# A hybrid decoder layer: one batch of row gathers cut four shorter, a Gelu in two halves, and other places for gathers and matmul chunks

## The chip, the cores and the metric

The kernel runs on one core of a Trainium2 chip. The number compared is device time in microseconds (us), taken over whole executions. The kernel before was timed three times: 1535.12, 1538.91 and 1541.09 us, median 1538.91 us. One further execution was profiled, and all rows below come from it.

The core's engines each work through their own list of instructions in order and meet at semaphores. PE multiplies matrices, DVE does element-wise work and reductions, ACT evaluates functions such as Exp, Ln and Gelu and copies results out of PE's accumulators, POOL issues the indirect gathers, and SP issues most plain transfers.

## The reference

The input is 512 tokens of width 1024. A layer has two halves, each closed by a LayerNorm over `alpha * x + f(x)`.

- The mixing half projects x to queries, keys and values. Eight heads (group A) are softmax attention over dilated windows: Exp of scores, divided by its sum. Eight heads (group B) are stick-breaking attention: `exp(log_sigmoid(z) + later)`, where `later` sums `log_sigmoid(-z)` over the later keys. So B needs Exp and Ln.
- The channel half looks up single-neuron experts. For each token, 8 heads each pick 16 of 16384 experts (128 in all, with softmax gates). Then

```
h   = einsum('td,ted->te', xb, u)        # u = rows of expert_u, 128 per token
act = gate * gelu(h, approximate=False)
y   = einsum('te,ted->td', act, vv)      # vv = rows of expert_v, 128 per token
```

## The kernel before

The 512 tokens are four blocks of 128. The channel half is computed in two ways:

- Blocks 0 and 1 gather. POOL fetches, for selection j of a block, one row of 1024 floats per token (512 KB in all). DVE uses it once: for `peer_u` rows it forms the dot product with x (L739, the result goes to column j of a tile `hs` of 128 columns), for `peer_v` rows it adds `hs[:, j] * row` to an accumulator (L750). A block has 128 gathers of u, then Gelu of `hs` (L741), a product with the gates (L745), then 128 gathers of v. Two blocks make 512 gathers. The generator `gathers` issues each up to 8 ahead of its use, and `done` counts uses.
- Blocks 2 and 3 are dense. PE multiplies x with all experts, 128 chunks of 128 (`h_part`, L847: 8 matmuls a chunk, each of which the trace shows as 2 records), ACT takes Gelu (L839), DVE multiplies with gates that were scattered to a dense table, and PE multiplies with `peer_v` (L1104). Up to 30 chunks (LEAD) are done ahead of the last loop, by `run_ahead(n)`, n matmuls at a time.

The order in time is this. First come the input projection and block 0's attention and routing (choice of its experts). Then `early = gathers(PRE0)` is mixed with the rest of the projection and with the A heads of blocks 1 and 2. From there on the order is written out by hand (`tc.manual_schedule()`):

1. The head pipeline: A heads of block 3, B heads of blocks 1, 2 and 3. One A head is scores on PE (L315), mask and minimum on DVE (L318), Exp on ACT (L321), transposes on PE (L325), a copy on ACT (L328), the product with v on PE (L331). One B head is scores on PE (L339, L341), Abs, Exp and Ln on ACT (L345, L346, L347), a sum on DVE (L349), sums over keys on PE (L351, L353), Exp on ACT (L355), the product with v on PE (L359). Heads overlap. `take(n)` puts n gather uses between the steps. The output projection and LayerNorm of blocks 1 and 2 are spread between the heads of blocks 2 and 3 (L497 on PE, L457 on DVE, then L160 on DVE, Ln and Exp on ACT at L161 and L162, L164 on DVE).
2. The output projection of block 3, then queries and scores of blocks 1 to 3 with DVE's top-16 searches, `run_ahead(1)` per step.
3. `route_steps(2)`, the routing of block 2, on DVE in 23 pieces, with gather uses and `run_ahead(8)` between the pieces. Near its end ACT takes an Exp (L681). It closes with three transposes on PE (L709).
4. The one-hot loop of 64 steps: DVE makes one-hot tiles (L798, L804), ACT scales them by the gates (L813), PE multiplies them (L819), and ACT copies the result out (L825). Beside it go gather uses, routing of blocks 3 and 1, and `run_ahead(2)` per step (3 in every eighth).
5. Chunks that are left of the 30, each with three gather uses, then the last loop over 128 chunks, in which the gathers that are left are spread.

ACT's functions come from tables. L176 loads one at the start, named `natural_log_exp_and_others`. After that the build puts an ACT_TABLE_LOAD ahead of a function that the table loaded last lacks, and the program and the trace show it under that function's line: the kernel before has 14 of them, one at L176, the next at L741.

Of the kernel before, what the change touches and what calls it, by code (L numbers as in the profile page):

```python
# [15 lines left out]
AF = mybir.ActivationFunctionType  # L16
# [57 lines left out]
LEAD = 30  # L74
KT = 6
MIXB = (5, 4, 2)
PRE0 = 68
QGATH = 3
QH = 1
PRE1 = 7  # L80
# [13 lines left out]
def build(ctx, nc, tc, a):  # L94
# [323 lines left out]
    def until(main, side, ratio):  # L418
        n = 0
        for _ in main:  # L420
            n += 1
            while n >= ratio:
                n -= ratio
                next(side, None)
# [5 lines left out]
    def run(*steps):  # L430
        ratio = steps[-1] if isinstance(steps[-1], tuple) else (1,) * len(steps)
        for _ in mix(*steps[:len(ratio)], ratio):
            pass

    def mix(*steps):
        ratio = steps[-1]
        live = [(s_, r) for s_, r in zip(steps, ratio)]
        while live:
            for s_, r in list(live):
                for _ in range(r):  # L440
                    if next(s_, s_) is s_:
                        live.remove((s_, r))
                        break
                    yield

    def head(steps, n):
        for _ in range(n):
            if next(steps, steps) is steps:
                return
            yield  # L450
# [283 lines left out]
    def gather_use(n, u):  # L734
        tb, kind, j = n // (2 * P), n // P % 2, n % P
        gate_, hs = sets[tb]
        x = x2[:, tb]
        if kind == 0:
            nc.vector.scalar_tensor_tensor(u, u, 1.0, x, op0=OP.mult, op1=OP.mult, accum_out=hs[:, j:j + 1])  # L739
            if j == P - 1:  # L740
                nc.scalar.activation(hs, hs, AF.Gelu)  # L741
                nc.vector.tensor_scalar_mul(x, x, ALPHA)
            return
        if j == 0:
            nc.vector.tensor_mul(hs, hs, gate_)  # L745
        if j == 1:
            nc.vector.tensor_scalar_mul(yg[0], u, hs[:, j:j + 1])
        else:
            acc = (x, yg[0])[j % 2]
            nc.vector.scalar_tensor_tensor(acc, u, hs[:, j:j + 1], acc, op0=OP.mult, op1=OP.add)  # L750
        if kind and j == P - 1:
            nc.vector.tensor_add(x, x, yg[0])
# [4 lines left out]
    def gathers(n):  # L757
        nonlocal done, issued
        while done < n:
            ahead_ = GB1 + GB2 if g2 else GB1  # L760
            while issued < min(done + ahead_ - 1, limit):
                gus[issued] = gather(issued)
                issued += 1
            gather_use(done, gus.pop(done))
            done += 1
            yield
# [27 lines left out]
    def one_hot_b(s):  # L794
        if s < NS:
            tb, t = steps[s]
            hot1[s] = gb.tile([P, P, TG], BF16, name="o1b", bufs=GBUF)
            nc.vector.tensor_tensor(hot1[s], gate[tb][0][:, None, t:t + TG].to_broadcast([P, P, TG]), iob, op=OP.is_equal)  # L798
# [32 lines left out]
    def load_u(c):  # L831
        if c < P:
            us[c] = wst.tile([P, KD, P], F32, name="w", bufs=WBUF)
            nc.sync.dma_start(us[c], a["uT"][c])

    def gelu(c, ps):
        if c % 2 == 0:
            gls[c // 2] = up.tile([P, 2, ND], F32, name="gl", bufs=LEAD // 2 + 2)
        nc.scalar.activation(gls[c // 2][:, c % 2], ps[:, :ND], AF.Gelu)  # L839
# [3 lines left out]
    def h_part(c, k0, k1):  # L843
        if k0 == 0:
            hps[c] = ps_h.tile([P, 512], F32, name="h", bufs=2)
        for k in range(k0, k1):
            nc.tensor.matmul(hps[c][:, :ND], us[c][:, k], xf[:, k], start=k == 0, stop=k == KD - 1)  # L847
        if k1 == KD:
            del us[c]
# [8 lines left out]
    def run_ahead(n):  # L858
        out = None
        for _ in range(n):  # L860
            nxt_ = next(ahead, None)
            if nxt_ is None:
                break
            c, k = nxt_
            if c == k == 0:
                for i in range(3):
                    load_u(i)
            if k == 0:
                load_u(c + 3)
                if c and c - 1 in hps:  # L870
                    out = c - 1
            h_part(c, k, k + 1)
        if out is not None:
            gelu(out, hps.pop(out))
# [15 lines left out]
    rest = []  # L890
    limit = PRE0 + GB1 - 1
    early = gathers(PRE0)
    until(mix(route_steps(0, 4, 4), head(early, PRE1), (2, 1)), proj, 1)
# [14 lines left out]
    gs = gathers(NG)  # L908
# [14 lines left out]
    with tc.manual_schedule():  # L923
        def take(n):
            for _ in head(gs, n):
                pass
# [40 lines left out]
                fill = chain(fill, project_out(fill_at), normalize(fill_at))  # L967
        for g_ in after:
            for _ in g_:
                pass  # L970
        for _ in fill:
            pass
        qs.close()
# [43 lines left out]
        nc.vector.tensor_copy(iob, iota[:, :, None].to_broadcast([P, P, TG]))  # L1017
        load_g(0)
        for i, _ in enumerate(route_steps(2)):
            if i % 3 == 0:  # L1020
                run_ahead(KD)
            elif i % 3 == 1:
                run(head(gs, 1))
        run_ahead(KD)
        run_ahead(KD)
        one_hot_b(0)
        one_hot_b(1)
        gated(0)
# [207 lines left out]
```

## Time and profile before

| what | value |
|---|---|
| median of three runs | 1538.91 us |
| the profiled execution | 1538.36 us, its span 1536.6 us |
| PE busy | 1413.3 us (92%) |
| DVE busy | 1199.4 us (78%) |
| ACT busy | 513.7 us (33%) |
| POOL busy | 684.2 us (45%) |
| moved by DMA | 495.95 MB, mean 323 GB/s |
| clock granted to PE, mean over the span | 0.939 of full speed |

A busy share is a mean over stages with different limits, so a stage has to be read by itself. The waits in the timeline stand in brackets: how long an engine was idle before the instruction, and what ended that. Matmuls overlap, and their ends are modelled, so PE shows 100% also where it is not at its peak. Times in the rows count from the span's start.

### The profile page before, as it was taken

To read this page: it belongs to the slowest core of one execution; us is meant where nothing else is said; L and a number is where in the kernel's file an instruction comes from. 1 tells how busy PE (TensorE), PEld (TensorE's weight loads), DVE (VectorE), ACT (ScalarE), POOL (GpSimd) and SP (SyncE) were. 2 spreads that over 40 slices of the span, in tenths; PEclk is the share of its full clock that TensorE was granted. 3 is DMA by queue.
4 is the path that set the end of the run, shared out by engine and by line. 5 is a ranking of instruction groups with operands and counts; after the bars stand their busy time and mean duration, and the time that the engine had idled before them with its cause. 6 is when DMAs were issued, how large, how long until landed. Compare 5 with 4: busy or idle time off the path is not lost.

```text
span 1536.6 us, 19753 instructions
## 1 busy us (share of the span) xinstructions
PE 1413.3 (92%) x6686; PEld 1140.0 (74%) x6686; DVE 1199.4 (78%) x2473; ACT 513.7 (33%) x1072; POOL 684.2 (45%) x526
## 2 busy tenths in 40 slices
PE   7989888899998999299989999999999999999896
PEld 3658676667665999298768888888878887878685
DVE  0138888855777999989988877778778888888987
ACT  1422333344432111189962222222222222222351
POOL 0000376743483433201537655555555656666400
PEclk9889998956998999699999999999999999999998
DMA  8657799894688998557999999999999999999972
GB/s 291 219 170 240 268 343 320 283 360 151 190 296 328 328 335 295 186 173 221 333 332 371 409 409 410 410 410 409 410 409 410 409 410 410 410 409 407 397 257 84
DMA packets 163221, 495.95 MB, mean 323 GB/s; under 512 B 15376, under 2 KB 48288, under 8 KB 163120
## 3 DMA queue, kind: packets, MB, share of 16 engines
q0 software_dynamic: 74304, 270.13, 47.2%
q1 hardware_dynamic: 86432, 218.66, 38.8%
q10 hardware_dynamic: 2384, 5.90, 1.0%
q8 instruction: 53, 0.87, 0.2%
q14 instruction: 48, 0.39, 0.1%
HBM read 477.78 MB, written 16.84 MB: 322 GB/s over the span
## 4 chain that ended last, share of the span: by engine, by line
DMA 35%; PE 32%; DVE 12%; issue 11%; POOL 6%; ACT 3%; SPq 0%; POOLq 0%; ACTq 0%; DVEq 0%
DMA g<-peer_u,eidx 18%; DMA g<-peer_v,eidx 14%; POOL g L730 6%; PE y L1104 4%; PE h L847 3%; PE a L597 2%; PE b L597 2%; PE m L262 2%; PE m L497 1%; DVE g L739 1%; DVE vl L124 1%; PE h L331 1%; ACT o L813 1%; PE h L359 1%; PE h L566 1%
## 5 line engine op out<-in xcount | busy, mean ns | idle before, releaser
L730 POOL DMA_INDIRECT g<-peer_u,eidx x256 | 335.9, 1312 | 405.6 <-DVE topi L542 146.1
L730 POOL DMA_INDIRECT g<-peer_v,eidx x256 | 342.5, 1338 | 352.5 <-DVE yg L750 107.6
L847 PE MATMUL h<-xf,w 128*128 128x256 f32 x2048 | 475.4, 381 | 11.7 <-ACT gl L839 11.7
L847 PEld LDWEIGHTS h<-xf,w 128*128 128x128 f32 x2048 | 384.8, 191 | 64.5 <-ACT gl L839 12.1
L739 DVE SCALAR_TENSOR_TENSOR g<-g,x 128x1024 f32<-128x1024 f32 x256 | 308.2, 1222 | 82.4 <-DMA g<-peer_u,eidx 81.8
L1104 PE MATMUL y<-vh,a 128*128 128x512 f32 x928 | 288.7, 415 | 14.4 <-ACT a L1090 13.0
L1104 PEld LDWEIGHTS y<-vh,a 128*128 128x128 f32 x928 | 173.3, 190 | 61.0 <-ACT a L1090 19.5
L750 DVE SCALAR_TENSOR_TENSOR x<-g,hg,x 128x1024 f32<-128x1024 f32 x128 | 163.8, 1280 | 22.8 <-DMA g<-peer_v,eidx 22.3
L750 DVE SCALAR_TENSOR_TENSOR yg<-g,hg,yg 128x1024 f32<-128x1024 f32 x126 | 161.1, 1279 | 22.0 <-DMA g<-peer_v,eidx 21.1
L124 DVE TENSOR_TENSOR vl<-v,vh 128x1024 fp32r<-128x1024 f32 x122 | 148.9, 1221 | 21.6 <-ACT vh L1059 21.1
L1090 ACT ACTIVATE a<-gl 128x512 fp32r<-128x512 f32 x58 | 36.5, 629 | 372.7 <-DVE gl L1084 372.7
L1104 PE MATMUL y<-vl,a 128*128 128x512 f32 x464 | 147.6, 400 | 8.9 <-DVE vl L124 8.9
L1059 ACT ACTIVATE vh<-v 128x1024 fp32r<-128x1024 f32 x122 | 128.4, 1053 | 27.9 <-PE y L1104 17.4
L1104 PEld LDWEIGHTS y<-vl,a 128*128 128x128 f32 x464 | 86.4, 190 | 33.2 <-DVE vl L124 14.7
L839 ACT ACTIVATE gl<-h 128x256 f32<-128x256 f32 x128 | 47.9, 375 | 136.7 <-PE h L847 133.6
L813 ACT ACTIVATE o<-o1b,sg 128x128 f32<-128x128 bf16 x256 | 83.4, 400 | 1.6 <-DVE o1b L798 1.4
L262 PE MATMUL m<-w,x0f 128*128 128x256 f32 (+1 forms) x128 | 48.4, 520 | 9.0 <-DMA x0f<-xT 7.8
L128 PE MATMUL m<-wl,x2h 128*128 128x512 f32 x96 | 42.4, 442 | 12.0 <-DVE wl L124 11.9
L819 PEld LDWEIGHTS m<-o,o 128*128 128x128 f32 x304 | 39.5, 195 | 11.8 <-issue 4.4
L819 PE MATMUL m<-o,o 128*128 128x128 f32 x304 | 42.0, 282 | 5.6 <-DVE o L804 4.5
L804 DVE TENSOR_TENSOR o<-sg,c_small 128x512 f32<-128x512 f32 x64 | 44.0, 687 | 0.9 <-PE b L819 0.4
L262 PEld LDWEIGHTS m<-w,x0f 128*128 128x128 f32 x128 | 24.1, 200 | 26.3 <-issue 11.4
(261 smaller groups left out, 1920.4 us busy)
## 6 DMA issues: line engine op xcount, KB each, us to landing
w<-uT SPq DMA_DIRECT2D x128, 512.0 KB
v<-peer_v SPq DMA_DIRECT2D x128, 512.0 KB
w<-w_in SPq DMA_DIRECT2D x47, 512.0 KB
gt<-gd SPq DMA_DIRECT2D x15, 960.0 KB
w<-peer_wq SPq DMA_DIRECT2D x16, 512.0 KB
wq<-peer_wq SPq DMA_DIRECT2D x16, 512.0 KB
gd<-stage SPq DMA_DIRECT2D x15, 512.0 KB
gd<-stage SPq DMA_DIRECT2D x15, 448.0 KB
```

The lines of the kernel that those rows point to most:

```text
L124: nc.vector.tensor_sub(parts[1], src, parts[0].bitcast(F32))
L262: nc.tensor.matmul(ps[:, ch * wd:(ch + 1) * wd], x0f[:, kk], w[:, k], start=kk == 0, stop=kk == KD - 1)
L597: nc.tensor.matmul(qps[it][:, (lo - 1) * P:(hi - 1) * P], w, xf[:, kk, (lo - 2) * P:(hi - 2) * P], start=False, stop=kk == KD - 1, skip_gr ...
L730: nc.gpsimd.indirect_dma_start(out=u, out_offset=None, in_=a["peer_v" if kind else "peer_u"], in_offset=bass.IndirectOffsetOnAxis(ap=eidx[ ...
L739: nc.vector.scalar_tensor_tensor(u, u, 1.0, x, op0=OP.mult, op1=OP.mult, accum_out=hs[:, j:j + 1])
L750: nc.vector.scalar_tensor_tensor(acc, u, hs[:, j:j + 1], acc, op0=OP.mult, op1=OP.add)
L813: nc.scalar.activation(hot[s][:, j], o1b[:, :, j], AF.Copy, scale=gate[tb][1][:, 1, t + j:t + j + 1])
L819: nc.tensor.matmul(gps[s][:, j * P:(j + 1) * P], o2[:, j], o1[:, j], start=True, stop=True)
L839: nc.scalar.activation(gls[c // 2][:, c % 2], ps[:, :ND], AF.Gelu)
L847: nc.tensor.matmul(hps[c][:, :ND], us[c][:, k], xf[:, k], start=k == 0, stop=k == KD - 1)
L1059: nc.scalar.activation(vsp[c][0], vs[c], AF.Copy)
L1104: nc.tensor.matmul(yps[t][hf], s_, w_[:, hf * 512:(hf + 1) * 512], start=c == 0 and n == 0, stop=c == P - 1 and n == len(terms) - 1)
```

## The change

Five edits:

- PRE0 goes from 68 to 64: the generator `early` ends four gather uses sooner.
- Gelu of `hs`, and the product with the gates, are done for columns 0 to 63 and 64 to 127 apart. The first Gelu comes right after use 64 of a block, the first product just before the first use of a v row, and the second product before the 65th use of a v row.
- While the last head's closing steps run at the end of the pipeline, each is followed by one gather use (two in all).
- Beside `route_steps(2)`, `run_ahead(8)` is called at every second piece where it was every third: 12 calls for 8, that is four chunks more. A gather use stays at every third piece.
- After these and two more calls of `run_ahead(8)`, three gather uses are added ahead of the first one-hot tiles.

```diff
-PRE0 = 68
+PRE0 = 64
...
         if kind == 0:
             nc.vector.scalar_tensor_tensor(u, u, 1.0, x, op0=OP.mult, op1=OP.mult, accum_out=hs[:, j:j + 1])
+            if j % 64 == 63:
+                nc.scalar.activation(hs[:, j - 63:j + 1], hs[:, j - 63:j + 1], AF.Gelu)
             if j == P - 1:
-                nc.scalar.activation(hs, hs, AF.Gelu)
                 nc.vector.tensor_scalar_mul(x, x, ALPHA)
             return
-        if j == 0:
-            nc.vector.tensor_mul(hs, hs, gate_)
+        if j % 64 == 0:
+            nc.vector.tensor_mul(hs[:, j:j + 64], hs[:, j:j + 64], gate_[:, j:j + 64])
...
         for g_ in after:
             for _ in g_:
-                pass
+                take(1)
...
         for i, _ in enumerate(route_steps(2)):
-            if i % 3 == 0:
+            if i % 2 == 0:
                 run_ahead(KD)
-            elif i % 3 == 1:
-                run(head(gs, 1))
+            if i % 3 == 1:
+                take(1)
         run_ahead(KD)
         run_ahead(KD)
+        take(3)
```

The instructions move with it. Names in the rows are tiles, a number behind a name tells copies of it apart, and line numbers behind the edits are one or two higher in the new kernel.

On DVE, where `early` ends and the hand-written order begins: `g` are gathered rows, `x_97` is block 0's x, `o<-h,rz` closes block 2's A heads, and `su,nm<-a,c_maska 128x512` is the mask step of block 3's first head. Before:

```order
L739 SCALAR_TENSOR_TENSOR g,hg<-g,x_97 128x1024 x3
L364 RECIPROCAL rz<-z 128x8
L739 SCALAR_TENSOR_TENSOR g,hg<-g,x_97 128x1024
L365 TENSOR_TENSOR o<-h,rz 128x512
L739 SCALAR_TENSOR_TENSOR g,hg<-g,x_97 128x1024 x3
L318 ISA su,nm<-a,c_maska 128x512
L318 ISA nm 128x1
```

Now:

```order
L739 SCALAR_TENSOR_TENSOR g,hg<-g,x_97 128x1024 x3
L364 RECIPROCAL rz<-z 128x8
L365 TENSOR_TENSOR o<-h,rz 128x512
L318 ISA su,nm<-a,c_maska 128x512
L318 ISA nm 128x1
```

Four gather uses that stood ahead of the head's first DVE step now stand behind it.

On ACT, in the head pipeline, where block 1's LayerNorm (L161, L162) passes between two B heads of block 2 (`su` is a head's tile, `m` and `a` are accumulators). Before:

```order
L345 ACTIVATE su<-m_2771 128x384
L346 ACTIVATE su<-su 128x384
L347 ACTIVATE su<-su,ones 128x384
L161 ACTIVATE lw<-lw 128x1
L162 ACTIVATE lw<-lw 128x1
L355 ACTIVATE su<-a 128x384
```

Now:

```order
L345 ACTIVATE su<-m_2760 128x384
L346 ACTIVATE su<-su 128x384
L347 ACT_TABLE_LOAD
L347 ACTIVATE su<-su,ones 128x384
L161 ACTIVATE lw<-lw 128x1
L162 ACT_TABLE_LOAD
L162 ACTIVATE lw<-lw 128x1
L355 ACTIVATE su<-a 128x384
```

Here two loads are added. The whole order of ACT has 64 of them now, 50 more: one for the first Gelu, one for the Exp behind it, and 48 in the head pipeline, wherever ACT goes from Exp to Ln or back. In the order of before the first load after the start stands at L741, behind the last B head.

On PE, between the end of block 2's routing (L709) and the first one-hot product (L819): `h<-xf,w` are the chunk matmuls. Before:

```order
L608 MATMUL m_4166<-skT,qT 128x128 x3
L847 MATMUL h<-xf,w 128x256 x66
L709 MATMUL tr<-c_ident,i_4389 128x128
L709 MATMUL tr<-c_ident,i_4390 128x128
L709 MATMUL tr<-c_ident,gate 128x128
L847 MATMUL h<-xf,w 128x256 x16
L819 MATMUL a<-o_4528,o_4533 128x128 x4
```

Now:

```order
L608 MATMUL m_4161<-skT,qT 128x128 x3
L848 MATMUL h<-xf,w 128x256 x90
L709 MATMUL tr<-c_ident,i_4398 128x128
L709 MATMUL tr<-c_ident,i_4399 128x128
L709 MATMUL tr<-c_ident,gate 128x128
L848 MATMUL h<-xf,w 128x256 x24
L820 MATMUL a<-o_4583,o_4588 128x128 x4
```

Of the 32 matmuls that move, 24 go ahead of the transposes and 8 go between them and the first one-hot product.

## Rows read from the trace of the kernel before

A timeline row is start, duration, engine, line, operation, tiles, shapes, count, and in brackets the idle time before it and what ended it.

**Rows 1.** Page, part 4: the chain that ended last, shares by engine.
```profile
DMA 35%; PE 32%; DVE 12%; issue 11%; POOL 6%; ACT 3%; SPq 0%; POOLq 0%; ACTq 0%; DVEq 0%
```

**Rows 2.** Windows: us, busy of PE, PEld, DVE, ACT, POOL; clock, DMA share, GB/s.
```profile
302.00:310.00 8.00, 0.53 (x4) 0.42 (x3) 3.67 (x7) 1.41 (x3) 5.19 (x5) 0.64 0.98 363
310.00:372.00 62.00, 61.28 (x211) 46.24 (x210) 29.92 (x61) 25.07 (x59) 24.93 (x22) 0.50 0.71 265
372.00:401.00 29.00, 28.31 (x128) 18.34 (x127) 16.26 (x29) 10.66 (x21) 11.62 (x10) 0.99 0.60 184
401.00:412.00 11.00, 9.10 (x50) 7.14 (x49) 10.49 (x23) 5.62 (x12) 3.46 (x3) 0.84 0.41 124
412.00:436.00 24.00, 24.00 (x147) 19.04 (x147) 21.67 (x37) 15.82 (x26) 18.91 (x14) 1.00 0.82 265
636.00:651.00 15.00, 0.80 (x3) 0.54 (x4) 14.59 (x26) 0.00 (x0) 3.96 (x3) 0.50 0.37 107
651.00:661.00 10.00, 10.00 (x38) 8.23 (x36) 4.46 (x17) 2.26 (x8) 1.21 (x1) 0.76 0.52 160
716.00:792.00 76.00, 72.59 (x454) 61.38 (x453) 75.42 (x179) 70.88 (x202) 39.06 (x19) 1.00 0.98 320
806.00:1430.00 624.00, 612.16 (x2725) 510.78 (x2724) 507.41 (x646) 152.50 (x244) 373.16 (x273) 1.00 1.02 407
```

**Rows 3.** Timeline of DVE, 296 to 309 us.
```profile
297.67 1.22 DVE L739 SCALAR_TENSOR_TENSOR g<-g,x 128x1024 f32<-128x1024 f32 x1
306.83 1.23 DVE L739 SCALAR_TENSOR_TENSOR g<-g,x 128x1024 f32<-128x1024 f32 x1 [2.95 <-DMA g<-peer_u,eidx]
307.98 0.69 DVE L318 CUSTOM_DVE_ANT_0 su<-a,c_maska 128x512 f32<-128x512 f32 x1
```

**Rows 4.** Timeline of PE, 300 to 310 us.
```profile
300.44 0.59 PE L315 MATMUL b<-kA,qA 64*128 64x512 f32 x1
301.39 0.66 PE L173 MATMUL tr<-c_ident,o 128*128 128x128 f32 x4
309.58 1.12 PE L325 MATMUL a<-c_ident,su 128*128 128x128 f32 x4 [7.47 <-issue]
```

**Rows 5.** Timeline of ACT, 300 to 309 us.
```profile
300.00 0.60 ACT L394 ACTIVATE x<-tr 128x512 f32<-128x512 f32 x1
308.71 0.72 ACT L321 ACTIVATE su<-su,nm 128x512 f32<-128x512 f32 x1 [6.03 <-DVE nm L318]
```

**Rows 6.** Timeline of ACT, 461 to 469 us.
```profile
461.33 1.28 ACT L741 ACT_TABLE_LOAD   x1
462.62 0.31 ACT L741 ACTIVATE hg<-hg 128x128 f32<-128x128 f32 x1
462.95 1.28 ACT L161 ACT_TABLE_LOAD   x1
467.25 1.28 ACT L162 ACT_TABLE_LOAD   x1
```

**Rows 7.** Timeline of ACT, 403 us.
```profile
403.23 0.20 ACT L162 ACTIVATE lw<-lw 128x1 f32<-128x1 f32 x1
```

**Rows 8.** Timeline of PE, 460 us.
```profile
460.51 1.88 PE L497 MATMUL tr<-wo,xf 128*128 128x512 f32 x4
```

**Rows 9.** Timeline of DVE, 462 to 466 us.
```profile
462.96 0.29 DVE L745 TENSOR_TENSOR hg<-hg,gate 128x128 f32<-128x128 f32 x1 [6.79 <-ACT hg L741]
465.16 0.68 DVE L457 SCALAR_TENSOR_TENSOR x<-x,tr 128x512 f32<-128x512 f32 x1
```

**Rows 10.** Timeline of PE, 611 to 661 us.
```profile
611.66 9.44 PE L847 MATMUL h<-xf,w 128*128 128x256 f32 x43
651.13 9.38 PE L847 MATMUL h<-xf,w 128*128 128x256 f32 x32
```

**Rows 11.** Timeline of DVE, 661 us.
```profile
661.28 0.42 DVE L798 TENSOR_TENSOR o1b<-s,iob 128x512 bf16<-128x512 bf16 x1 [5.78 <-ACT o L813]
```

**Rows 12.** Timeline of DVE, 799 us.
```profile
799.02 1.23 DVE L124 TENSOR_TENSOR vl<-v,vh 128x1024 fp32r<-128x1024 f32 x1 [3.67 <-ACT vh L1059]
```

## The prediction

> **What bounds the kernel now.** The chain that ended last is mixed: DMA 35%, PE 32%, DVE 12%, ACT only 3% [rows 1]. Such shares hide stages, so I went to the windows by stage next [rows 2], and to the timelines of the places that the change touches last. The windows show three regimes. In the last loop (806 to 1430) the DMA share is 1.02 at 407 GB/s: the bytes still to be moved set its length, and whatever starts it late ends it late. In the one-hot loop's second half (716 to 792) DVE is busy 75.42 of 76 us. In the head pipeline PE fills the time: 61.28 of 62 us from 310 to 372, at half clock (0.50, that is 1.2 GHz), then 28.31 of 29 and 24.00 of 24, at or near full clock. ACT has 25.07, 10.66 and 15.82 us of work in these three, so it looks free. That is where the reader should look twice, because the order of ACT is where this change adds most.
>
> **The table loads.** The diff only cuts a Gelu in two and moves its first half ahead of the head pipeline. But a Gelu replaces the table that held Exp and Ln together. Once it is gone, Exp and Ln get a table each: already before, behind the Gelu, the Ln of L161 and the Exp of L162 each have a load of their own [rows 6]. The new order of ACT has 50 loads more: one for the early Gelu, one for the Exp behind it, 48 between Exp and Ln in the pipeline. A load is 1.28 us, and the next instruction starts 0.01 us after it (461.33 to 462.61, then 462.62) [rows 6].
>
> I lay them beside ACT's work, stage by stage [rows 2], placing each load by its neighbours in the order:
> - 310 to 372: 17 loads, 25.07 + 21.8 = 46.9 us of 62. It fits, behind a PE at half clock. Cost 0.
> - 372 to 401: 11 loads, 10.66 + 14.1 = 24.8 of 29. Fits. Cost 0.
> - 401 to 412: 4 loads, 5.62 + 5.1 = 10.7 of 11. Full but just fits. However, block 1's LayerNorm passes here, and it is a chain: Ln, then Exp (at 403.23 [rows 7]), then DVE, then PE's transposes. Two of the four loads now stand in this chain one after the other, the one of L347 ahead of the Ln and the one of L162. 2 x 1.28 = 2.6. Bounds 0 (other work covers it) and 5.1 (all four count); I take 2.6.
> - 412 to 436: 12 loads, 15.82 + 15.4 = 31.2 of 24. Doesn't fit, and ACT works in order, so it becomes the bound: +7.2. Bounds 0 (the heads' overlap swallows it) and 15.4 (every load is exposed); I take 7.2, the surplus.
> - From 436 on: four loads in 28 us in which PE also does the output projection. Cost 0.
>
> The loads make +9.8. Against this reading stands one page: the Trainium skill (ScalarE: Activation LUTs, section "What ACT_TABLE_LOAD costs") puts a switch at about 2.66 us, 1283 ns for the load and 1380 ns for a drain. Its first figure is that of the rows; the drain isn't seen in them. By the page the four windows would overrun by 8, 11, 5 and 24 us, and the sum below would be some 38 us higher.
>
> **The start of the pipeline.** DVE's step for block 3's first head (L318) stood behind a gather use that waited 2.95 us for its data, and came at 307.98 [rows 3]. PE then sat idle for 7.47 us until 309.58 [rows 4]. Four uses go from in front of it: the last one left ahead ran at 297.67 [rows 3]. The scores end at 300.44 + 0.59 = 301.0 [rows 4], so L318 can end at 301.7. What is late next is ACT. The early Gelu enters ahead of the copy that started at 300.00 [rows 5]: load 1.28 and Gelu 0.31 [rows 6] to 301.6, the copy 0.60 to 302.2, PE's transposes 0.66 [rows 4] to 302.9, the second copy 0.60 to 303.5, and the load for Exp 1.28 to 304.8. The Exp starts then, where it started at 308.71 [rows 5]: -3.9. Bounds: -7.5 (the whole idle time of PE) and 0.
>
> PE's clock fell in this gap (a mean of 0.64 over 302 to 310, then 0.50 [rows 2]). PE still has a gap of about 2.7 us (302.9 to 305.6) and soon waits for ACT's first slow steps, so I let it fall as before.
>
> **The end of the pipeline.** DVE waited 6.79 us at L745 for the Gelu, which stood on ACT behind the last head's Exp; block 2's second half L457 came behind that, at 465.16 [rows 9]. Its input from PE was there at 460.51 + 1.88 = 462.4 [rows 8]. Now L457 has only u uses ahead: -2.8. The second Gelu and its load (1.6 us) now stand ahead of ACT's copy for the last head; PE's transposes cover about 1 us of it: +0.6. Together -2.2. The two uses added here (1.2 us each) fill the time in which DVE waited: 0.
>
> **Chunks beside the routing.** 32 matmuls move up. 24 go ahead of the closing transposes, into a stretch where PE is busy 0.80 of 15 us [rows 2]: 0. The other 8 go between these transposes and the first one-hot product, and ACT's Gelus of these chunks stand ahead of the first scaled one-hots. Here 32 records took 9.38 us, starting at a low clock (0.76 over 651 to 661 [rows 2]); at full clock 43 take 9.44, 0.22 each [rows 10]. 16 records more at 0.22 are 3.5 us, and DVE already waits 5.78 us for this ACT work [rows 11], so they are on the path: +3.5. Bounds: +1.2 (all 48 at 0.22) and +7 (the added ones at half clock). The three uses added on DVE (3.6 us) fit into its wait of 5.78: 0.
>
> **The one-hot loop.** 110 of the 240 matmuls done ahead are left at its start, where 136 were asked for, so its last 12 of 64 steps have none. DVE sets the pace there: 0. Were it PE, it would be 12 x 4 x 0.22 = -10.5; that is the lower end.
>
> **The last loop.** By the order of DVE, 222 gathers are used when it starts, where it was 224. Three uses that stood beside the last chunk are gone, at a place where DVE waits 3.67 us anyway [rows 12]: 0. Two gathers more in a loop bound by bytes: 2 x 0.524 MB at 407 GB/s = +2.6 (bounds 0 and 2.6). The halves of block 1's Gelu lie in this loop, with no table to load: 0.
>
> **Sum.** +9.8 - 3.9 - 2.2 + 3.5 + 2.6 = +9.8. The profiled execution took 1538.36 us, 0.55 below the median, so against the median: 1538.91 + 9.8 = 1548.7. I say 1549.
>
> **Rivals.**
> - A, PE's clock stays up at the start of the pipeline. For it: the gap shrinks from 7.5 to 2.7 us. Against: PE then waits for ACT again and again. PE would need 31 us from 310 to 372, ACT's 46.9 would decide, 15 us less than 62: 1534. Not slower.
> - B, the loads cost nothing. For it: several heads overlap, and from 436 on ACT has room. Against: in order, 31.2 us can't pass in 24. Without the +9.8: 1539. Not slower.
> - C, PE's clock falls between 412 and 436, since PE now waits there. 24 us at full clock are 48 at half, +24 where I have +7.2: 1566. Against: PE would still be busy about three quarters of the time.
> - D, a load holds ACT for longer than its row, say twice (2.57). The four windows overrun by 6.7, 9.9, 4.9 and 22.6, 44 where I have 9.8: 1583. Against: the 0.01 us in rows 6. This is the side on which the page with the drain stands.
>
> **How the numbers follow.** Forecast 0.56, A 0.12, B 0.15, C 0.13, D 0.04. About 0.5% (7.7 us: 1531.2 to 1546.6) is what a measurement of this kernel can tell from no change. The forecast's own range is 1541 to 1557: 0.44 slower, 0.12 within. A, with its bounds and a little of the one-hot loop's, is 0.05 faster and 0.07 within; B 0.03 faster and 0.12 within; C and D are slower. So faster 0.08, same 0.31, slower 0.61. The range runs from 1532 to 1567: it leaves out D, the upper half of C and the lower third of A.
>
> **What would show it.** 64 loads on ACT, most between Exp and Ln, 1.28 us each with the next instruction right behind. L318 of block 3's first head some 6 us sooner, its Exp some 4. PE at half clock behind that for 50 us or more. Where block 3's B heads run without other PE work, ACT nearly always busy and PE waiting for it. No wait of DVE for the Gelu at the pipeline's end. The first one-hot product some 3 us later after the routing's end than before. I am wrong if PE's clock stays up through the first heads, if PE shows no waits for ACT in the second part, or if the last loop starts no later than 806 us.

## The result, and the profile after

| | before | changed |
|---|---|---|
| median (12 runs each) | 1536.06 us | 1547.67 us |
| lowest to highest | 1529.05 to 1541.09 | 1544.74 to 1555.08 |
| profiled execution, its span | 1538.36, 1536.6 | 1548.69, 1546.9 |
| table loads on ACT | 14 | 64 |

The changed kernel takes 1.0074 times as long as the one before (95% interval 1.0057 to 1.0091): slower, where 1549 us was forecast. Between the two profiled executions lie 10.3 us, where the sum had +9.8. In the ratios below, runs over 1.5% above the fastest of their kernel are left out, which drops two of e9_whole's twelve and five of e2_seam's six and none elsewhere.

The first fence is the page of the changed kernel, part 4 [rows 1], the second its windows [rows 2] (columns as there).

```profile
DMA 33%; PE 30%; DVE 21%; issue 7%; ACT 6%; POOL 2%; SPq 0%; ACTq 0%; POOLq 0%; DVEq 0%
```

```profile
302.00:310.00 8.00, 4.92 (x21) 3.97 (x21) 4.43 (x9) 7.88 (x14) 6.47 (x6) 0.65 0.98 382
310.00:372.00 62.00, 61.78 (x210) 45.48 (x210) 25.09 (x51) 45.27 (x72) 18.96 (x17) 0.52 0.66 235
372.00:401.00 29.00, 27.95 (x130) 18.37 (x128) 19.07 (x35) 23.68 (x33) 11.03 (x10) 1.00 0.55 175
...
412.00:436.00 24.00, 21.36 (x122) 16.20 (x121) 16.49 (x28) 23.58 (x30) 14.65 (x11) 1.00 0.74 252
...
806.00:1430.00 624.00, 609.16 (x2699) 509.29 (x2700) 507.04 (x648) 155.16 (x247) 368.07 (x270) 0.99 1.02 406
```

The chain's ACT share rose from 3% to 6% only. The windows say where it matters: from 412 to 436 ACT is busy 23.58 of 24 us (15.82 before) and PE fell from 24.00 to 21.36. From 310 to 372 ACT rose by 20 us as well, and PE is as full as before, at half clock.

The start of the pipeline, timelines of DVE, ACT and PE in the changed kernel [rows 3 to 5]:

```profile
296.74 1.22 DVE L739 SCALAR_TENSOR_TENSOR g<-g,x 128x1024 f32<-128x1024 f32 x1
...
299.13 1.28 ACT L741 ACT_TABLE_LOAD   x1
...
300.12 0.69 DVE L318 CUSTOM_DVE_ANT_0 su<-a,c_maska 128x512 f32<-128x512 f32 x1 [1.24 <-PE b L315]
...
302.53 1.28 ACT L321 ACT_TABLE_LOAD   x1
303.82 0.72 ACT L321 ACTIVATE su<-su,nm 128x512 f32<-128x512 f32 x1
...
304.69 1.11 PE L325 MATMUL a<-c_ident,su 128*128 128x128 f32 x4 [2.81 <-ACT su L321]
```

The use that ran at 297.67 before stands at 296.74, so all here is read 0.93 us sooner. L318 waits for PE's scores and for no gather. The Exp starts at 303.82 (304.75 on the time scale of before; 304.8 was forecast), and what is late is ACT with its two loads.

Block 1's LayerNorm, ACT [rows 7]. A load stands ahead of the head's Ln (L347), which the LayerNorm's Ln (L161) follows, and another ahead of its Exp (L162):

```profile
398.74 1.28 ACT L347 ACT_TABLE_LOAD   x1
400.04 0.61 ACT L347 ACTIVATE su<-su,ones 128x384 f32<-128x384 f32 x1
400.56 0.19 ACT L161 ACTIVATE lw<-lw 128x1 f32<-128x1 f32 x1
400.76 1.28 ACT L162 ACT_TABLE_LOAD   x1
402.06 0.20 ACT L162 ACTIVATE lw<-lw 128x1 f32<-128x1 f32 x1
```

One B head behind it, ACT and then PE: no idle time on ACT, and PE, with full clock, waits for its L355:

```profile
413.19 1.28 ACT L347 ACT_TABLE_LOAD   x1
414.49 0.72 ACT L347 ACTIVATE su<-su,ones 128x512 f32<-128x512 f32 x1
415.23 1.28 ACT L355 ACT_TABLE_LOAD   x1
416.52 0.49 ACT L355 ACTIVATE su<-m 128x384 f32<-128x384 f32 x1
...
417.06 0.88 PE L359 MATMUL h<-v,su 128*128 128x64 f32 x6 [0.61 <-ACT su L355]
```

How far the heads stand from those of before is read at PE's product L359. Three of them before, and the same three in the changed kernel:

```profile
402.57 0.78 PE L359 MATMUL h<-v,su 128*128 128x64 f32 x6
410.22 0.78 PE L359 MATMUL h<-v,su 128*128 128x64 f32 x6
441.53 1.00 PE L359 MATMUL h<-v,su 128*128 128x64 f32 x8
```

```profile
398.83 0.78 PE L359 MATMUL h<-v,su 128*128 128x64 f32 x6
409.50 1.13 PE L359 MATMUL h<-v,su 128*128 128x64 f32 x6
447.84 1.00 PE L359 MATMUL h<-v,su 128*128 128x64 f32 x8
```

They are 3.7 us sooner, then 0.7 sooner, then 6.3 later.

The end of the pipeline [rows 8, 9]; the first line is the last head's Exp before, the others are the changed kernel. DVE no longer waits for the Gelu; but the second half's Gelu now waits for the last use on DVE, and block 3's copy L394 and PE wait behind it:

```profile
460.71 0.60 ACT L355 ACTIVATE su<-m 128x512 f32<-128x512 f32 x1 [5.89 <-issue]
...
467.03 0.60 ACT L355 ACTIVATE su<-m 128x512 f32<-128x512 f32 x1 [5.89 <-PE m L353]
...
468.75 0.69 DVE L457 SCALAR_TENSOR_TENSOR x<-x,tr 128x512 f32<-128x512 f32 x1 [4.13 <-PE tr L497]
...
476.33 0.26 ACT L741 ACTIVATE hg<-hg 128x64 f32<-128x64 f32 x1 [2.20 <-DVE g L739]
...
476.50 0.58 ACT L394 ACTIVATE xf<-tr 128x512 f32<-128x512 f32 x1
...
477.13 1.12 PE L173 MATMUL tr<-c_ident,x 128*128 128x128 f32 x4 [3.13 <-ACT xf L394]
```

Routing to the end [rows 10 to 12]: the chunks ahead of the first one-hot product, the first product into y, and the first of the four closing sums:

```profile
656.22 12.10 PE L848 MATMUL h<-xf,w 128*128 128x256 f32 x48
668.23 1.38 PE L820 MATMUL a<-o,o 128*128 128x128 f32 x8
...
809.43 1.22 PE L1106 MATMUL y<-vh,a 128*128 128x512 f32 x2 [6.45 <-ACT a L1092]
...
1529.34 0.69 DVE L1120 SCALAR_TENSOR_TENSOR w<-x,y 128x512 f32<-128x512 f32 x1 [1.98 <-PE y L1106]
```

Nine such moments cut each profiled execution into stages, in us: S the start of block 1's closing transposes (PE L173); a to block 3's first PE L331; b to block 1's second L457; c to its LayerNorm's Exp (L162); d to block 2's second L457; e to the first product of the query stage (L595); f to the routing's last transpose (L709); g to the first product into y; h to the first of the four closing sums (DVE `w<-x,y`), which the expectations call the last sum. "Uses" are the gather uses done when the last loop starts, by the order of DVE.

| kernel | S | a | b | c | d | e | f | g | h | uses |
|---|---|---|---|---|---|---|---|---|---|---|
| before | 299.4 | 14.5 | 85.9 | 3.45 | 61.9 | 24.6 | 161.1 | 150.7 | 717.4 | 224 |
| changed | 298.4 | 10.0 | 87.6 | 6.02 | 66.7 | 25.9 | 161.4 | 153.4 | 719.9 | 222 |
| e1_reload | 295.2 | 8.7 | 88.2 | 3.46 | 62.2 | 27.1 | 161.4 | 152.6 | 722.2 | 222 |
| e7_midreload | 295.4 | 10.0 | 90.0 | 3.46 | 59.0 | 27.1 | 161.4 | 152.6 | 718.6 | 222 |
| e2_seam | 289.6 | 6.8 | 83.0 | 3.45 | 62.2 | 24.2 | 161.2 | 150.9 | 723.8 | 220 |
| e4_route | 291.0 | 16.2 | 88.2 | 3.45 | 68.1 | 24.5 | 161.2 | 153.1 | 718.7 | 224 |
| e9_whole | 293.3 | 6.8 | 84.0 | 3.46 | 59.3 | 27.3 | 161.1 | 154.2 | 721.0 | 222 |
| e10_best | 292.1 | 6.8 | 88.5 | 3.46 | 62.2 | 24.2 | 161.1 | 150.2 | 717.9 | 224 |
| e5_nolate | 299.2 | 10.0 | 87.3 | 6.02 | 66.5 | 25.7 | 161.4 | 151.3 | 719.6 | 222 |
| e6_take5 | 297.9 | 10.0 | 89.4 | 6.02 | 65.9 | 27.2 | 161.4 | 152.6 | 716.6 | 224 |
| e11_pad | 293.6 | 10.1 | 88.0 | 3.46 | 65.4 | 27.1 | 161.2 | 152.4 | 722.7 | 222 |

S, b and d scatter by some us between executions of like code (e4_route runs the code of before up to the routing, and its S is 8.4 us sooner, its d 6.2 longer, with PE's clock low for longer); c and f hardly scatter. Up to 8 us ahead of S, PE, DVE and ACT go through the same instructions in all eleven profiles, and the last thirty of PE's take 4.6 us in each, so S is no effect of any edit: of the 13.9 us by which e2_seam's profiled span is shorter than that of before, 9.8 lie ahead of S.

### The profile page after: what moved, and what is told of

Read it like the earlier page. It is cut to its first block, busy times and chain, and to the rows that moved or that the text cites. A ratio compares the mean times of both kernels' runs of the same rounds, so it can differ in the third digit from the quotient of the medians.

```text
span 1546.9 us, 19807 instructions
## 1 busy us (share of the span) xinstructions
PE 1422.2 (92%) x6686; PEld 1147.8 (74%) x6686; DVE 1200.4 (78%) x2475; ACT 578.3 (37%) x1124; POOL 686.6 (44%) x526
## 4 chain that ended last, share of the span: by engine, by line
DMA 33%; PE 30%; DVE 21%; issue 7%; ACT 6%; POOL 2%; SPq 0%; ACTq 0%; POOLq 0%; DVEq 0%
DMA g<-peer_u,eidx 15%; DMA g<-peer_v,eidx 15%; PE y L1106 6%; PE h L848 6%; DVE yg L751 3%; DVE x L751 3%; POOL g L730 2%; PE m L262 2%; DVE o L805 2%; PE m L497 1%; PE tr L497 1%; DMA v<-peer_v 1%; PE h L331 1%; ACT o L814 1%; PE h L566 1%
## 5 line engine op out<-in xcount | busy, mean ns | idle before, releaser
L730 POOL DMA_INDIRECT g<-peer_u,eidx x256 | 339.8, 1327 | 407.2 <-DVE topi L542 145.9
L1061 ACT ACTIVATE vh<-v 128x1024 fp32r<-128x1024 f32 x122 | 128.4, 1054 | 29.0 <-PE y L1106 13.9
L1106 PEld LDWEIGHTS y<-vl,a 128*128 128x128 f32 x464 | 87.3, 191 | 28.2 <-DVE vl L124 9.3
L820 PE MATMUL m<-o,o 128*128 128x128 f32 x304 | 45.8, 301 | 9.5 <-ACT o L814 5.8
L820 PEld LDWEIGHTS m<-o,o 128*128 128x128 f32 x304 | 43.1, 212 | 14.7 <-ACT o L814 9.5
```

The source lines that it names most:

```text
L730: nc.gpsimd.indirect_dma_start(out=u, out_offset=None, in_=a["peer_v" if kind else "peer_u"], in_offset=bass.IndirectOffsetOnAxis(ap=eidx[ ...
L820: nc.tensor.matmul(gps[s][:, j * P:(j + 1) * P], o2[:, j], o1[:, j], start=True, stop=True)
L1061: nc.scalar.activation(vsp[c][0], vs[c], AF.Copy)
L1106: nc.tensor.matmul(yps[t][hf], s_, w_[:, hf * 512:(hf + 1) * 512], start=c == 0 and n == 0, stop=c == P - 1 and n == len(terms) - 1)
```

## The experiments

Times beside each are medians of the kernel and of the kernel before on the same chip; the ratio, which isn't the quotient of these two medians, is told with its 95% interval.

**e1_reload.** The changed kernel, with

```diff
+            if i == 0:
+                nc.scalar.preload_act_table_set("natural_log_exp_and_others")
```

> The changed kernel with one line more: at step 0 of the head pipeline, behind the early Gelu, the table that holds Exp and Ln together is loaded again, so ACT has 14 table loads instead of 64 and none between Exp and Ln. Theory (the loads are what the change costs, where ACT has no room for them): the time falls by the +9.8 of the forecast, from 1547.7 to about 1538; if the lags between the two traces are taken instead of the forecast's terms (1.8 from 310 to 372 us, 3.0 up to 410, 9.4 up to 434, 2.4 of it given back until 460), by 11.8, to about 1536. The windows 412 to 436 of ACT fall back from 23.6 of 24 us to about 16. Rival B (the loads cost nothing, the time went to the chunks and the last loop): about 1547.7, and the same milestones as the changed kernel.

Measured 1540.18 against 1538.22, ratio 1.0020 (1.0001 to 1.0039). Of the 0.74% that the change costs, 0.54% go with the reload: 8.3 us by the ratios, 9.7 by the medians. Its window:

```profile
412.00:436.00 24.00, 24.00 (x133) 17.65 (x133) 21.97 (x38) 14.84 (x25) 19.23 (x13) 1.00 0.75 239
```

ACT is back at 14.84 us and PE at 24.00; c is back at 3.46. Rival B falls, since the intervals of the two ratios lie apart. The forecast's +9.8 for the loads lies within what they leave open, some 4 to 12 us.

**e7_midreload.** The same two lines with `i == 18`.

> The changed kernel with the shared Exp and Ln table loaded again at step 18 of the head pipeline (about 377 us): the loads beside a PE at half clock stay (some 27), those behind it go. Theory (a load costs only where ACT with its loads has more work than the stage lasts): as the run with the reload at step 0, within 2 us, so 1536 to 1540; the lag of the heads at 372 us stays that of the changed kernel, and no further lag is built up from 401 to 436. Rival (every load costs its 1.28 us or some fixed part of it, wherever it stands): about half of the gain of the earlier reload, so 1542 to 1543.

Measured 1539.81 against 1538.22, ratio 1.0013 (0.9994 to 1.0031): no worse than the reload at step 0, though it has 23 loads more (37 against 14).

```profile
310.00:372.00 62.00, 61.77 (x208) 45.86 (x207) 26.81 (x54) 45.26 (x72) 19.15 (x16) 0.51 0.62 221
...
412.00:436.00 24.00, 24.00 (x133) 17.71 (x133) 21.85 (x38) 14.96 (x25) 19.23 (x13) 1.00 0.77 249
```

From 310 to 372 ACT has 45.26 us of work and PE stays full: loads beside a PE at half clock are hidden, as far as the runs can tell (some 4 us either way). A fixed price per load is out: half of the gain would stand at 1.0047, above the interval.

**e2_seam.** The kernel before, with

```diff
-PRE0 = 68
+PRE0 = 64
```

> The kernel before with PRE0 = 64 alone: Gelu whole and behind the heads, one-hot stage and routing as before. Theory: the first score of block 3 no longer waits for gathers, so the heads begin earlier: without the early Gelu and its two loads ahead of the Exp, PE's first transpose comes some 6 us sooner than at 309.58 (the forecast gave -3.9 with the loads in the way); DVE's wait of 6.79 us at the pipeline's end goes too (-2.8). Four gathers fewer are used by the last loop, which is bound by bytes: 4 x 1.3 = +5.2. Sum -3.6 to -5.6 with the loads' 1.3 to 2 us not in the way: 1530.5 to 1532.5. Rival (the seam's gain is lost again because PE's clock is low there and the heads wait for other things): the heads' lead is gone by 372 us, and with the four gathers the time is 1538 to 1541.

Its six runs spread from 1501.69 to 1538.21 (median 1529.57 against 1538.22), too far for an interval. I hadn't expected the spread. The median is 8.7 us below before, more than the 3.6 to 5.6 of the theory; against the rival, no run lies above the median of before, but six runs this far apart settle no more than the direction. Stage a fell from 14.5 to 6.8. PE's clock fell only near 307 us here, and was back at 355, where the kernel before has half clock from 304 to 372:

```profile
302.00:310.00 8.00, 6.24 (x31) 4.80 (x31) 5.13 (x10) 4.46 (x11) 4.01 (x4) 0.83 1.03 410
310.00:372.00 62.00, 61.31 (x222) 43.91 (x222) 30.96 (x58) 23.55 (x51) 22.24 (x19) 0.64 0.66 236
```

Over the runs the time goes with the mean granted clock: 1501.69 at 0.964, 1524.48 at 0.949, 1538.21 at 0.938. An estimate from these: over 1501.69 us, 0.964 makes some 108 us at half clock, and the profiled run (1524.48) had 156. The 48 us between them are as many as that run spent at half clock from 307 to 355, but without a trace of the fastest run it isn't shown that this is the stretch that it lacks. Stage h grew by 6.4 with four uses fewer (5.2 expected).

**e4_route.** The kernel before with only the third part of the diff (from `if i % 2 == 0:` to `take(3)`).

> The kernel before with only the third part of the change: the H chunks beside block 2's routing at every second step, gather uses at every third, and three uses behind it. Theory: the first one-hot product comes 2.7 to 3.5 us later behind the routing's end than before (48 matmuls instead of 32 ahead of it); the one-hot loop keeps its length, since DVE sets its pace. Uses by the last loop are two more than in the kernel before, which is worth -2.6 there. Sum 0 to +1: 1536 to 1537. Rival (the one-hot loop gains what its last 12 steps no longer do on PE, 10 us): 1526 to 1529. Second rival (the chunks are no cost, as they would have been done anyway): 1533.

Measured 1539.56 against 1538.22, ratio 1.0015 (0.9997 to 1.0032). The count of uses in the expectation was mine and wrong: it has 224, as before, so nothing was to be gained in the last loop, and 1541 to 1542 was the right sum. The rival with 10 us from the one-hot loop falls. The second rival (the chunks cost nothing) would now stand at 1.0000, which the interval holds; against it speaks stage g, which grew by 2.3.

**e9_whole.** The changed kernel with only the cut of the Gelu undone:

```diff
-            if j % 64 == 63:
-                nc.scalar.activation(hs[:, j - 63:j + 1], hs[:, j - 63:j + 1], AF.Gelu)
             if j == P - 1:
+                nc.scalar.activation(hs, hs, AF.Gelu)
```

(and the product with the gates whole at j == 0).

> The changed kernel with only the cut of the Gelu undone: block 0's Gelu runs whole after its last u product, behind the heads, so ACT has no load at the start of the pipeline and none between Exp and Ln; PRE0 = 64, the chunks beside the routing and the uses stay. 222 uses by the last loop. Theory 1 (the early Gelu costs twice: its loads in the heads, about 8 us, and its own load and the one behind it at the start of the pipeline, which lengthen PE's gap there so that PE's clock falls there and stays low for some 65 us; without them the gap is 1.3 us and the low stretch some 48 us, as in the run with PRE0 = 64 alone): 0.995 to 0.998 of the kernel before (that run's 0.9944, plus 2.3 us for the chunks, less 2.6 for two uses). Theory 2 (the clock falls at this place whatever the gap, and only the loads matter): as the run with the reload at step 0, less 1.3 to 2.6 us for the load ahead of the Exp: 1.000 to 1.002 of the kernel before.

Measured 1533.60 against 1537.66, ratio 0.9956 (0.9924 to 0.9988): theory 1's value, and under all of theory 2's. The means of all twelve runs and of before stand at 0.9965, theory 1's value still. Undoing the cut turns 0.74% slower into 0.35 to 0.44% faster, twice what the loads in the heads cost. Runs went down to 1515.85, at a mean clock of 0.959; e1_reload's twelve lie from 1535.78 to 1543.56, at 0.937 to 0.942.

**e10_best.** The kernel before, with PRE0 = 64 and

```diff
         run_ahead(KD)
         run_ahead(KD)
+        run(head(gs, 4))
         one_hot_b(0)
```

> The kernel before with PRE0 = 64 and four gather uses more behind block 2's routing, where DVE waited 5.6 us for ACT in the run with PRE0 alone; Gelu whole, chunks as before. 224 uses by the last loop, where the run with PRE0 alone has 220. Theory (a use that is not done by the last loop is paid there by its bytes, 1.3 us each; four uses of 1.2 us fit into DVE's wait): 5.2 us less than with PRE0 alone, so about 0.991 of the kernel before, with the same spread from run to run, and 717 to 719 us from the first product into y to the last sum instead of 723.8. Rival (the last loop's length is not set by the count of uses left): as with PRE0 alone, 0.994.

Measured 1524.15 against 1537.66, ratio 0.9895 (0.9863 to 0.9928): faster than the kernel before and than the changed one. The theory's 0.991 lies in the interval, the rival's 0.994 doesn't. Timelines of PE at the start of the pipeline and at the first product into y, and of DVE at the first closing sum:

```profile
296.12 0.66 PE L325 MATMUL a<-c_ident,su 128*128 128x128 f32 x4 [1.33 <-ACT su L321]
...
788.47 1.22 PE L1105 MATMUL y<-vh,a 128*128 128x512 f32 x2 [4.88 <-ACT a L1091]
...
1506.34 0.69 DVE L1119 SCALAR_TENSOR_TENSOR w<-x,y 128x512 f32<-128x512 f32 x1 [2.76 <-PE y L1105]
```

PE waits 1.33 us there instead of 7.47 [rows 4]. Stage h is 717.9, against 723.8 with four uses fewer.

**e5_nolate.** The changed kernel, with

```diff
-            if i % 2 == 0:
+            if i % 2 == 0 and i < 22:
```

> The changed kernel without the chunk of H that it adds ahead of the first one-hot product (32 matmuls there again, as before, instead of 48); everything else stays, the loads too. Theory (these matmuls stand in the path from the routing's end to the first one-hot product, and the one-hot loop, which DVE sets, doesn't give them back): 2.7 us less than the changed kernel, 1.0056 of the kernel before; from the routing's last transpose to the first product into y 150.7 us, where the changed kernel has 153.4. Rival (PE has them to do anyway): 1.0074 and 153.4.

Measured 1544.62 against 1537.66, ratio 1.0043 (1.0022 to 1.0064). The predicted 1.0056 lies in it, and the 1.0074 of no effect doesn't; but the interval of that 1.0074 begins at 1.0057, so the time alone doesn't decide. The routing's end does:

```profile
656.40 8.60 PE L848 MATMUL h<-xf,w 128*128 128x256 f32 x32
664.90 1.38 PE L820 MATMUL a<-o,o 128*128 128x128 f32 x8
```

32 records (16 matmuls) take 8.60 us here, where 48 took 12.10; stage g is 2.1 shorter.

**e6_take5.** The changed kernel with `take(5)` in place of `take(3)`.

> The changed kernel with five gather uses behind block 2's routing instead of three, so 224 uses by the last loop as before, instead of 222. DVE waits 4.80 us for ACT there. Theory (2 x 1.3 us in the last loop): 1.0057 of the kernel before; from the first product into y to the last sum 717.4 us, where the changed kernel has 719.9; the way from the routing's end to the first product into y stays 153.4. Rival (these 2.6 us come from elsewhere in the last loop): 1.0074 and 719.9.

Measured 1544.45 against 1537.66, ratio 1.0043 (1.0024 to 1.0061). The predicted 1.0057 lies in it; again the time alone doesn't decide. Stage h is 716.6, where 717.4 was expected and 719.9 was the rival's, and g didn't grow.

**e11_pad.** e9_whole, with

```diff
+            if i == 0:
+                for _ in range(9):
+                    nc.scalar.activation(hg1, ident, AF.Copy)
```

> The kernel with the Gelu whole (0.9956 of the kernel before), and at the start of the pipeline, ahead of the first Exp of block 3, nine small copies on ACT (128x128, into a tile that is written again later), which hold that Exp up by some 2 us, as the early Gelu and its two loads did (first product of block 3's first head 8.7 us behind the first transpose of block 1's outputs in the run with the reload, 6.8 with the Gelu whole). No table load in it. Theory (it is PE's longer gap at this place that costs, through PE's clock: 9.8 us between these two runs, of which 2 by the gap itself): close to the run with the reload, 1.000 to 1.002 of the kernel before, and no execution under 1528 us. Rival (it is the loads or the Gelu themselves that cost those 9.8 us, somewhere else): 0.9956 plus the 2 us, so 0.997, with executions under 1520 us among them.

Measured 1536.54 against 1537.46, ratio 0.9991 (0.9976 to 1.0006), between the two, with runs from 1531.73 to 1543.31. ACT's copies, and PE's wait:

```profile
296.84 3.03 ACT L943 ACTIVATE hg<-c_ident 128x128 f32<-128x128 f32 x9
...
300.63 1.11 PE L325 MATMUL a<-c_ident,su 128*128 128x128 f32 x4 [4.27 <-ACT su L321]
```

The copies held the path up by 3.3 us (a is 10.1 instead of 6.8), where 2 was expected, and the time rose by 0.35%, 5.4 us (0.28% by the means, with all twelve runs of e9_whole). With 3.3 us in place of 2, the rival comes to 0.9977, just inside the interval, so the ratio doesn't separate the two. What does speak for the theory is that the executions under 1530 are gone (three of twelve in e9_whole), and the mean clocks over all kernels. PE's wait is the one ahead of the first head's L325; half clock is the stretch that begins there or soon behind, by the windows of the profiled execution:

| kernel | PE's wait, us | half clock, us | runs at a mean clock of 0.95 or more |
|---|---|---|---|
| e2_seam | 1.33 | 307 to 355 | 1 of 6 |
| e9_whole | 1.33 | 302 to 357 | 2 of 12 |
| e10_best | 1.33 | 298 to 363 | 2 of 6 |
| changed | 2.81 | 304 to 369 | 0 of 12 |
| e1_reload | 2.81 | 303 to 367 | 0 of 12 |
| e11_pad | 4.27 | 299 to 367 | 0 of 12 |
| before | 7.47 | 304 to 372 | 0 of 74 |

e5_nolate, e6_take5, e7_midreload (2.81 or 2.82) and e4_route (8.01) have none in 47 runs. So no execution with the longer gap, not even one made by harmless work, shows the high mean clock, and 5 of 24 with the short gap do. The short gap alone doesn't keep the clock up, as windows of e9_whole and then of e10_best show behind the same wait (granted clock 1.00, then 0.50):

```profile
298.00:302.00 4.00, 3.18 (x19) 2.13 (x19) 2.44 (x6) 3.62 (x10) 3.24 (x3) 1.00 0.99 383
...
299.00:302.00 3.00, 3.00 (x10) 2.12 (x10) 1.20 (x3) 1.47 (x4) 2.39 (x3) 0.50 1.02 415
```

e11_pad doesn't reach e1_reload's 1.0020, though its gap is longer: some 4.5 us between these two stay unexplained.

## Why the prediction was right

The sum was +9.8, the two profiled executions differ by 10.3, the medians by 11.6. That 1549 came so near to 1547.67 owes something to luck: over twelve runs the median of the kernel before is 1536.06, 2.85 below the one that the forecast started from, and the change cost 1.8 more. By its steps:

- **The table loads**, +9.8 forecast. c grew by 2.57, where 2 x 1.28 was forecast; across it PE's products L359 lost 3.0 us (from 3.7 sooner to 0.7 sooner). From 410 to 442 they lost 7.0, where 7.2 was the surplus. Together 10.0 in this pair; the runs of e1_reload say 8.3 by the ratios. Nothing from 310 to 372 that the runs can tell, as forecast (e7_midreload). The longer hold that would have brought rival D isn't there: the Ln starts 0.02 us behind its 1.28 us load (413.19 to 414.49). Rival C's fall isn't there either: from 412 to 436 the granted clock is 1.00.
- **The start**, -3.9 forecast; a shrank by 4.5. That PE's clock would fall here all the same was right for this kernel. Its reason was named too loosely: with the early Gelu's loads PE waits 2.81 us and the clock falls there; without them it waits 1.33, and in some executions the clock stays up for longer (e2_seam, e9_whole), in others not (e10_best). So rival A, at 0.12, was no outcome of this change but sits right beside it, and may be worth some 23 us in a single run (1501.69 against 1524.48, both of e2_seam). That the gap has a part in it is supported by e11_pad and the mean clocks; its size is not settled.
- **The end of the pipeline**, -2.2 forecast. DVE's wait for the Gelu is gone: L457 stands 1.7 us behind the last head's L355, where it stood 4.5 behind (-2.7; -2.8 forecast). The +0.6 for the Gelu ahead of the last copy was too small, and the 0 for the two uses in the closing steps was wrong, because I priced the Gelu's load and not what the Gelu waits for, the last use on DVE. In this pair e grew by 1.2; it is 27.1 to 27.3 in five of the seven kernels with uses in the closing steps (25.7 and 25.9 in the others), 24.2 to 24.6 without. e9_whole and e11_pad, with the Gelu whole, are among the five, so the cut isn't the cause.
- **The chunks**, +3.5 forecast. Seven profiles with 48 records of chunk matmuls ahead of the first one-hot product have a mean g of 153.0, four with 32 have 150.8: +2.2, near the lower bound of 1.2 to 7. PE's clock was back sooner: its mean was 0.87 over the 12.10 us of the 48 records, 0.25 us each, and 0.75 over the 9.38 us of the 32 before, 0.29 each.
- **The one-hot loop**, 0 forecast, and g leaves no room for more.
- **The last loop**, +2.6 forecast; h grew by 2.5. Over all kernels the mean is 717.6 at 224 uses, 720.7 at 222, 723.8 at 220: 1.5 us for a use, where 1.3 was taken; single profiles with 222 uses lie from 718.6 to 722.7.

## What to carry to other kernels

Before an activation function is moved on ACT, look at which table it evicts and who uses that table next: one Gelu ahead of a loop of Exp and Ln turned 14 loads into 64, and one line that reloads the shared table took 8 us back. Price such a load by the stage: here nothing that could be measured beside a PE at half clock, and all of it in a LayerNorm's chain and where ACT had no slack. And judge an edit by its parts: here a table of stages showed two good ones (the earlier start, and uses put into a real wait of DVE) under two bad ones, and the good ones alone took 1.05% off (e10_best, six runs).

## What the runs showed of the hardware that was not expected

- The time of one kernel can spread with TensorE's mean granted clock. With a gap of 1.3 us at the pipeline's start, e9_whole's runs went from 1515.85 (mean clock 0.959) to 1542.50 (0.939); with 2.8 us or more, in e1_reload and e11_pad, from 1531.73 to 1543.56. That the clock behind this gap makes the spread is likely by the profiles, and not shown, since no run at 0.95 or more was profiled.
- The same instructions reach the same place at other times: S lies between 289.6 and 299.4 us in these profiles, with stretches of half clock ahead of it that come and go: over the first 280 us the mean clock is 0.91 in before and 0.96 in e2_seam. A difference of single profiles in stages b and d says little below 5 us here.
